# One hybrid block on one core: the output projection as one accumulation of 12 k tiles beside attention and 4 after it

## The chip, the cores and the metric

The kernel runs on one core of a Trainium2 chip. A core has a matrix engine (PE, with its weight loads shown as PEld), a vector engine (DVE), a scalar engine (ACT), a general engine (POOL) and a queue engine (SP) that only issues transfers; transfers are also issued by POOL and ACT. The five run side by side, each in the order of its own instruction list, and meet only at semaphores. The metric is the device time of one execution in microseconds (us): lower is better.

## The reference

The block normalises its input, projects it, runs a state-space mixer (SSD) and a sparse attention side by side, joins their outputs, and projects the joined rows back onto the residual stream. Then a gated feed-forward part and a last normalisation follow. Shapes: 512 positions, model width 2048, SSD and attention 1024 each, feed-forward 5632, all in float32.

```python
u = rmsnorm(h, attn_norm_w)
z, xbc, dt_raw, q, kc, vc, ks, vs, kw, vw, gate_raw = split(u @ w_in)
y_ssd = ssd_mixer(...)        # ends in rmsnorm(y * silu(z), ssd_norm_w)
y_att = nsa_mixer(...)        # 16 heads: compressed, selected and windowed keys
mixed = concatenate([y_ssd, y_att], axis=-1)
h = h + mixed @ w_out                      # the projection of this case
v = rmsnorm(h, ffn_norm_w)
h = h + (silu(v @ w_gate) * (v @ w_up)) @ w_down
return rmsnorm(h, final_norm_w)
```

## The kernel before

Activations lie transposed: a tile holds 128 channels by 512 positions. `mixed` is 16 such k tiles: 8 of SSD (`P2["ms"]`) and 8 of attention (`P2["ma"]`). Each float32 operand is split into a rounded part (`hi`, made by ACT in `a_hi`) and a rest (`lo`, made by DVE). A product of one k tile is three PE instructions: hi with hi, hi with lo, lo with hi.

The first phase is a list of *units* (`run_unit`, L232 to L234). A unit makes one block of 128 output channels: it sums its k tiles into one PSUM bank `ps_g` (two banks take turns). Its weights come through `wp`, a pool with rings of four buffers: SP loads 4 k tiles (256 KB) into `wraw`, ACT makes `whi`, DVE makes `wlo`. After every k tile the code calls `sch.tick()`, and background tasks (generators) get to add their next instructions: the attention heads of group after group, the evictions of earlier units, and so on. What the code writes in this phase is then ordered by the planner of the language, engine by engine, from its own estimate of times; only from the feed-forward part on does the order stand as written.

The projection is cut in two.

- **Units over the SSD half.** The last 16 units (one for each 128 output channels) sum the 8 SSD k tiles, `w_out[c][:, 0:8]`, while the last attention group runs as a background task. `pre_out` runs before the first of them: it loads the gated SSD rows from `gy_d`, multiplies by the norm weight `C_SN` and splits them into `ms`. The division by the root mean square of a position, `row2`, is left to the eviction `ev_os`: DVE multiplies the PSUM block by `row2` into a tile `h1`, POOL's queue adds the residual `xT` in a transfer, and a second transfer writes it to `h1_d`. `ma_in` meanwhile reads back from `at_d` the attention tiles that were finished earlier.
- **Steps over the attention half.** When all tasks are done, `pre_oa` closes the pools of attention (`att`), of the weights (`wp`) and of the constants (`c1`) and opens `ws` in their place: `A`, `Z` (raw weights, 48 slots of 128x128), `R` (split weights), `E`, `T`, `V0`. Then 16 steps (`run_step`, L1154 to L1156) sum the 8 attention k tiles, `w_out[c][:, 8:16]`. The eviction `ev_oa(c)` adds `h1` (read from `h1_d` into a ring of two tiles, `HH`), writes the sum to `h_d`, adds its square to `acc2`, weights it by `C_FN` and splits it into the operands of the feed-forward part. `load_h1(c + 2)` then reads the next `h1` into the tile that step c has just used, and a step's PSUM bank is free when the add of the step two before it is done.

Gate, up and down products follow in the feed-forward part, whose weights stream through `Z` to the end.

Of the kernel before, what the change touches and what calls it, by code (L numbers as in the profile page):

```python
# [8 lines left out]
F32 = mybir.dt.float32  # L9
# [14 lines left out]
          (0, 5), (7, 5), (1, 5), (6, 5), (2, 5), (7, 5), (5, 6), (0, 6), (3, 6), (4, 6), (1, 4), (6, 4), (2, 4),  # L24
          (0, 6), (2, 3), (6, 5), (7, 6), (5, 6), (3, 6), (4, 6), (1, 6)]
GRING = 7
KSUB = 4
PACE = [1]
LAG = 3
# [83 lines left out]
def body(ctx, tc, xT, w_in, w_out, w_gate, w_up, w_down, w1k, w1v, cols, rows, kst, out):  # L113
# [53 lines left out]
    def open_pool(name, stack=None, **kw):  # L167
        es = ExitStack()
        pools[name] = (es, es.enter_context(tc.tile_pool(name=name, bufs=1, reuse_waits="tile", **kw)))
        return pools[name][1]  # L170
# [2 lines left out]
        pools.pop(name)[0].close()  # L173

    c1 = open_pool("c1")
    wp = open_pool("wp")


    subs = []
# [115 lines left out]
    up = right.enter_context(tc.tile_pool(name="up", bufs=1, side="right", reuse_waits="tile"))  # L295

    U = up.tile([128, 2, KD, 512], F32R, name="u")
    u_hi, u_lo = U[:, 0], U[:, 1]

    def u_rhs(k):  # L300
# [655 lines left out]
    def pre_out():  # L956
        sch.run_until(*[("gy", t) for t in range(8)])
        P2["ms"] = [(U[:, 0, k], U[:, 1, k]) for k in range(8)]
        P2["ma"] = [(U[:, 0, 8 + k], U[:, 1, 8 + k]) for k in range(8)]
        for k in range(8):  # L960
            w = col(C_SN + k)
            h_, l_ = P2["ms"][k]
            nc.sync.dma_start(f(l_), gy_d[k])
            a_hi(h_, f(l_), scale=w)
            dve.scalar_tensor_tensor(l_, f(l_), w, f(h_), op0=ALU.mult, op1=ALU.subtract)
        sch.add(ma_in(P2["at"] + 1))

    def ma_in(n):

        yield 8  # L970
        for k in range(n):
            h_, l_ = P2["ma"][k]
            nc.sync.dma_start(f(l_), at_d[k])
            yield 8
            a_hi(h_, f(l_))
            lo(dve, l_, f(l_), h_)

    def ev_os(c):
        def ev(p):
            yield from sch.wait("r2")  # L980
            t = pools["att"][1].tile([128, 512], F32, tag="qs", name="h1", bufs=2)
            mul(dve, t, p, P2["row2"])
            nc.gpsimd.dma_start(t, xT[c], accum_op=ALU.add)
            yield 4
            nc.gpsimd.dma_start(h1_d[c], t)
        return ev

    for c in range(KD):
        units.append(Unit(w_out[c][:, 0:8, :], 8, lambda k: P2["ms"][k], ev_os(c),
                          pre=pre_out if c == 0 else None))  # L990

# [168 lines left out]


    def pre_oa():
        sch.drain()
        close_pool("att")
        close_pool("wp")
        close_pool("c1")
        wsp = open_pool("ws")
        A = P2["A"] = wsp.tile([128, NA, 128], F32, name="A")  # L1170
        P2["T"] = {i: wsp.tile([128, 8, 2, 256], F32R, name=f"T{i}") for i in range(2)}
        P2["Z"] = wsp.tile([128, NZ, 128], F32, name="Z")

        P2["R"] = wsp.tile([128, 8 + NR * 128], F32R, name="R")[:, 8:].rearrange("p (k c) -> p k c", k=NR)
        tp = open_pool("ta", side="right")
        P2["V0"] = tp.tile([128, 8, 2, 256], F32R, name="V0")
        P2["VV"] = U[:, :, 0:8, :].rearrange("p a k (s t) -> p a k s t", s=2)
        at = 8
        for n, k in (("SR", 2), ("TT", 4), ("HH", 4), ("CT", 8), ("ST", 16)):
            P2[n] = A[:, at:at + 2 * k, :].rearrange("p (k a) t -> p k (a t)", a=2)  # L1180
            at += 2 * k
        P2["T34"] = P2["ST"].rearrange("p (a k) t -> p a k t", a=2)
        P2["T2"] = P2["CT"]
        P2["T1"] = [P2["Z"][:, i:i + 8, :].rearrange("p (k a) t -> p k (a t)", a=2) for i in (NZ - 16, NZ - 8)]
        fz.busy[NZ - 16:] = [True] * 16

        P2["E"] = open_pool("E", side="right").tile([128, NE * 128 + 8], F32R, name="E")[:, 0:NE * 128].rearrange(
            "p (k c) -> p k c", k=NE)
        advance()
        load_h1(0)  # L1190
        load_h1(1)

    def load_h1(c):
        if c < KD:
# [3 lines left out]
    def ev_oa(c):  # L1198
        def ev(p):
            h = P2.pop(("h1", c))  # L1200
            add(dve, h, p, h)
            nc.gpsimd.dma_start(h_d[c // 2][:, 2 * (c % 2):2 * (c % 2) + 2, :].rearrange("p a t -> p (a t)"), h)
            t = P2["t", c % 2] = P2["TT"][:, 2 * (c % 2):2 * (c % 2) + 2].rearrange("p a t -> p (a t)")
            dve.tensor_scalar(t, h, col(C_FN + c), None, op0=ALU.mult)
            if c == 0:
                act.activation(acc2, h, AF.Square)
            else:
                q = ps_v()
                act.activation(q, h, AF.Square)
                add(dve, acc2, q, acc2)  # L1210
            k = c // 2
            if c % 2 == 0:
                a_hi(P2["V0"][:, k, 0, :], t[:, 0:256])
                lo(dve, P2["V0"][:, k, 1, :], t[:, 0:256], P2["V0"][:, k, 0, :])
            else:
                e = P2["t", 0]
# [5 lines left out]
                pool.tensor_tensor(P2["T34"][:, 0, k, :], e[:, 256:512], t[:, 256:512], ALU.subtract)  # L1222
# [33 lines left out]
        return get  # L1256

    for c in range(KD):
        b = Blk(8, 1, w_out[c][:, 8:16, :])
        loads.append(b)  # L1260
        Step(b, lambda k: P2["ma"][k], oa_psum(c),
             after=ev_oa(c))


# [400 lines left out]
    def down_before(v, n):  # L1665
        def before():
            if n == 1 and v:
                assert v < NJ - 2 or not any(fz.busy[NZ2:])
                load_h(v + 1)
                P2["A2"] = P2["A"][:, 70:76, :]  # L1670
            elif (v, n) == (0, 0):
                close_pool("E")
                load_h(1)
                P2["E2"] = P2["E"] = open_pool("E", side="right").tile([128, NE, 128], F32, name="E2")
        return before

    last = []
# [34 lines left out]
        done.update(((i, 1), s.i) for i in range(a, b))  # L1712

    def run_rest():
        pre_oa()
# [6 lines left out]
        for n in ("E", "ta", "ws"):  # L1722
            close_pool(n)
        right.close()

# [145 lines left out]
```

## Time and profile before

| what | value |
|---|---|
| three runs, median (lowest to highest) | 2243.71 us (2239.92 to 2244.08) |
| the profiled execution's own time | 2242.56 us |
| its span, first to last instruction | 2240.8 us |
| PE, DVE, ACT busy, share of the span | 97%, 80%, 52% |
| mean granted clock of PE | 0.987 |
| last matmul of a unit, first matmul of a step | 763.8 us, 793.8 us |

Busy is time in which the engine has an instruction in work; a busy PE can still run at half its clock, which the granted clock shows. A row of a group gives the count, the busy time, the mean ns of one, and behind the second bar the idle time of that engine just before them and what ended it. In names buffer numbers are left out: `h_d<-h` is the write to `h1_d` in `ev_os`, `A<-h_d` on SP the load of `h1`, and `h_d<-A` the write in `ev_oa`. The table's last row is from the trace in order of time.

### The profile page before, as it was taken

Reading aid. Unit: us, or ns where it says so; the run is one execution under the profiler, and the core shown is the slowest. Engines: PE = TensorE matmul, PEld = TensorE weight load, DVE = VectorE, ACT = ScalarE, POOL = GpSimd, SP = SyncE. Lnnn points to the kernel's source line nnn. Section 1 sums busy time; section 2 is a strip of 40 time slices with the busy share of each in tenths; the row PEclk is TensorE's granted clock in tenths of the full one; section 3 lists DMA queues with packets and bytes.
Section 4 is the critical chain, followed back from the end, with each engine's and each line's share of the span. In section 5 each row is a group of like instructions: output and inputs, shape, how many; then the busy total and the mean of one; then the engine's idle time right before and its main releaser. Section 6 shows DMA issues by size and latency. Waiting matters only on the chain. (4 is left out here: it accounts for less than half of the span.)

```text
span 2240.8 us, 34941 instructions
## 1 busy us (share of the span) xinstructions
PE 2166.9 (97%) x12892; PEld 1905.9 (85%) x12892; DVE 1795.5 (80%) x2838; ACT 1173.0 (52%) x1944; POOL 418.3 (19%) x432
## 2 busy tenths in 40 slices
PE   7999999999989989999999999999999899999996
PEld 5888888888878768888888888888888799999996
DVE  7799766678887656888888888888888798888897
ACT  4564446567666534655555555555556343433453
POOL 2011225133232124100000000000000122212232
PEclk8999999999999989999999999999999999999998
DMA  5222342222325365788878888788888969696975
GB/s 179 90 71 76 117 154 91 85 79 71 123 74 145 71 209 176 217 236 217 247 220 254 226 231 237 215 247 229 238 236 219 331 238 317 180 299 176 300 193 135
DMA packets 168555, 417.17 MB, mean 186 GB/s; under 512 B 16592, under 2 KB 23520, under 8 KB 168384
## 3 DMA queue, kind: packets, MB, share of 16 engines
q1 hardware_dynamic: 97472, 248.04, 33.4%
q0 software_dynamic: 28192, 80.91, 18.7%
q10 hardware_dynamic: 42720, 85.99, 10.6%
q8 instruction: 101, 1.65, 0.3%
q14 instruction: 70, 0.57, 0.1%
HBM read 353.80 MB, written 57.41 MB: 184 GB/s over the span
## 5 line engine op out<-in xcount | busy, mean ns | idle before, releaser
L122 ACT ACTIVATE R<-Z 128x1024 fp32r<-128x1024 f32 (+4 forms) x462 | 423.7, 932 | 463.6 <-DVE Z L134 317.5
L125 DVE TENSOR_TENSOR R<-Z,R 128x1024 fp32r<-128x1024 f32 (+4 forms) x370 | 391.7, 1067 | 24.1 <-ACT R L122 20.7
L232 PE MATMUL ps_g<-u,whi 128*128 128x512 f32 x720 | 286.0, 397 | 0.0
L234 PE MATMUL ps_g<-u,wlo 128*128 128x512 f32 x720 | 284.5, 395 | 0.0
L233 PE MATMUL ps_g<-u,whi 128*128 128x512 f32 x720 | 284.5, 395 | 0.0
L1150 PE MATMUL ps_s<-u,R 128*128 128x512 f32 (+1 forms) x1160 | 252.8, 348 | 5.2 <-ACT A L1357 5.0
L1150 PEld LDWEIGHTS ps_s<-u,R 128*128 128x128 f32 x1160 | 187.7, 188 | 36.9 <-ACT A L1357 10.2
L125 DVE TENSOR_TENSOR wlo<-wraw,whi 128x512 fp32r<-128x512 f32 x196 | 149.6, 765 | 65.1 <-ACT whi L122 64.3
L122 ACT ACTIVATE whi<-wraw 128x512 fp32r<-128x512 f32 x196 | 122.6, 626 | 136.2 <-PE ps_g L233 89.3
L234 PEld LDWEIGHTS ps_g<-u,wlo 128*128 128x128 f32 x720 | 135.7, 188 | 26.6
L232 PEld LDWEIGHTS ps_g<-u,whi 128*128 128x128 f32 x720 | 135.9, 189 | 25.4
L233 PEld LDWEIGHTS ps_g<-u,whi 128*128 128x128 f32 x720 | 135.8, 189 | 25.5
L134 DVE TENSOR_TENSOR A<-ps_g,A 128x512 f32<-128x512 f32 (+1 forms) x114 | 73.9, 654 | 78.1 <-PE ps_g L1150 38.9
L1150 PE MATMUL ps_t<-u,R 128*128 128x512 f32 (+1 forms) x600 | 131.5, 348 | 0.0
L1150 PE MATMUL ps_g<-u,R 128*128 128x512 f32 x584 | 131.3, 349 | 0.0
L1150 PE MATMUL ps_s<-T,R 128*128 128x512 f32 (+1 forms) x560 | 126.9, 352 | 1.7 <-DVE R L125 1.7
L1150 PE MATMUL ps_g<-T,R 128*128 128x512 f32 (+1 forms) x584 | 127.2, 349 | 0.2 <-DVE R L125 0.2
L1154 PE MATMUL ps_g<-u,R 128*128 128x256 f32 (+1 forms) x353 | 115.2, 326 | 10.6 <-ACT R L122 7.0
L1150 PE MATMUL ps_s<-V,R 128*128 128x512 f32 (+1 forms) x568 | 122.7, 347 | 0.0
L122 ACT ACTIVATE R<-A 128x1024 fp32r<-128x1024 f32 (+3 forms) x76 | 72.1, 949 | 96.5 <-DVE A L134 59.9
L125 DVE TENSOR_TENSOR E<-Z,R 128x1024 fp32r<-128x1024 f32 x92 | 112.1, 1218 | 5.6 <-ACT R L122 5.2
L1155 PE MATMUL ps_g<-u,R 128*128 128x256 f32 (+1 forms) x353 | 114.4, 324 | 0.0
(473 smaller groups left out, 5633.8 us busy)
## 6 DMA issues: line engine op xcount, KB each, us to landing
Z<-in_w_up SPq DMA_DIRECT2D x95, 512.0 KB, 5.3
Z<-in_w_gate SPq DMA_DIRECT2D x94, 512.0 KB, 6.6
wraw<-in_w_in SPq DMA_DIRECT2D x164, 256.0 KB, 2.6
g_d<-A ACTq DMA_DIRECT2D x22, 1792.0 KB, 15.2
Z<-in_w_gate POOLq DMA_DIRECT2D x38, 512.0 KB, 6.6
Z<-in_w_up POOLq DMA_DIRECT2D x38, 512.0 KB, 8.7
Z<-in_w_down SPq DMA_DIRECT2D x59, 320.0 KB, 5.9
Z<-in_w_down SPq DMA_DIRECT2D x41, 384.0 KB, 4.0
```

The costliest lines, as they stand in the source:

```text
L122: act.activation(dst, src, AF.Copy, scale=scale)
L125: eng.tensor_tensor(dst, src, f(hi), ALU.subtract)
L134: eng.tensor_tensor(o, a, b, ALU.add)
L232: pe.matmul(p, hi_t[i][:, j, :], ah, start=(k == 0), stop=False)
L233: pe.matmul(p, hi_t[i][:, j, :], al, start=False, stop=False)
L234: pe.matmul(p, lo_t[i][:, j, :], ah, start=False, stop=(k == u.nk - 1))
L1150: pe.matmul(o, w, x, start=start, stop=(k == n - 1 and o is q), skip_group_check=not fresh[0])
L1154: pe.matmul(q, h[:, k, :], ah, start=(k == 0), stop=False)
L1155: pe.matmul(q, h[:, k, :], al, start=False, stop=False)
```

## The change

- `NS = 12`: a unit of the projection now sums 12 k tiles, the 8 of SSD and the first 4 of attention (48 weight loads for the 16 units in place of 32); a step sums the last 4, in blocks of 256 KB.
- Since one sum now holds both halves, `row2` cannot wait for the eviction. `pre_out` applies it to the operand: one DVE instruction multiplies by the norm weight and by `row2`, ACT makes `hi`, and one more DVE instruction makes `lo`. The rows come through the ring `wraw` of `wp`. `ev_os` is then a copy by ACT, into one tile `yz` where two tiles `qs` took turns.
- `wp` lies at the other end of memory (on the right, beside `u`), so that it can stay open when the pools of the left end change.
- `pre_last` runs ahead of the last unit: it takes all of attention's remaining instructions, closes `att` and `c1`, opens `ws` and issues the first loads of the steps; `first_forms` splits the first two blocks 6 and 9 ticks into the last unit. `T` moves to the place of `wp` and `V0` and `E` to the left end.
- In `ev_oa` the weighting by `C_FN` moves from DVE (L1204) to ACT.

```diff
+NS = 12
...
-    wp = open_pool("wp")
...
+    wp = open_pool("wp", side="right")
...
         for k in range(8):
-            w = col(C_SN + k)
             h_, l_ = P2["ms"][k]
-            nc.sync.dma_start(f(l_), gy_d[k])
-            a_hi(h_, f(l_), scale=w)
-            dve.scalar_tensor_tensor(l_, f(l_), w, f(h_), op0=ALU.mult, op1=ALU.subtract)
+            t = wp.tile([128, 512], F32, tag="raw", name="gy", bufs=4)
+            nc.sync.dma_start(t, gy_d[k])
+            dve.scalar_tensor_tensor(t, t, col(C_SN + k), P2["row2"], op0=ALU.mult, op1=ALU.mult)
+            a_hi(h_, t)
+            lo(dve, l_, t, h_)
...
     def ma_in(n):
-        yield 8
         for k in range(n):
...
-            yield 8
+            yield 1 if k < NS - 8 else 8
...
     def ev_os(c):
         def ev(p):
-            yield from sch.wait("r2")
-            t = pools["att"][1].tile([128, 512], F32, tag="qs", name="h1", bufs=2)
-            mul(dve, t, p, P2["row2"])
+            if "att" in pools:
+                t = pools["att"][1].tile([128, 512], F32, tag="yz", name="h1", bufs=1)
+            else:
+                t = P2["TT"][:, 2 * (c % 2):2 * (c % 2) + 2].rearrange("p a t -> p (a t)")
+            act.activation(t, p, AF.Copy)
             nc.gpsimd.dma_start(t, xT[c], accum_op=ALU.add)
...
+    def pre_last():
+        sch.run_until(("a", 3), ("evac", st["unit"]))
+        pre_oa()
+        sch.add(first_forms())
+
+    def first_forms():
+        yield 6
+        prep(0)
+        yield 3
+        prep(1)
...
-        units.append(Unit(w_out[c][:, 0:8, :], 8, lambda k: P2["ms"][k], ev_os(c),
-                          pre=pre_out if c == 0 else None))
+        units.append(Unit(w_out[c][:, 0:NS, :], NS, os_rhs, ev_os(c),
+                          pre={0: pre_out, KD - 1: pre_last}.get(c)))
...
-            dve.tensor_scalar(t, h, col(C_FN + c), None, op0=ALU.mult)
+            a_hi(t, h, scale=col(C_FN + c))
...
-        b = Blk(8, 1, w_out[c][:, 8:16, :])
+        b = Blk(16 - NS, 1, w_out[c][:, NS:16, :])
...
-        Step(b, lambda k: P2["ma"][k], oa_psum(c),
+        Step(b, lambda k: P2["ma"][NS - 8 + k], oa_psum(c),
```

Three places in the built programs follow. The PE list is the same in both up to the start of the projection.

The first is ACT where attention ends and the steps begin. `fo<-ps_v` and `u<-at` belong to the last attention tile, and `R<-Z` is the first split of a step's weights. Before:

```order
L122 ACTIVATE pth<-ps_t 128x2x128
L122 ACTIVATE pth<-ps_t 128x3x128
L122 ACTIVATE pth<-ps_t 128x4x128
L884 ACTIVATE fo<-ps_v 64x512
L122 ACTIVATE u<-at 128x512
L122 ACTIVATE R<-Z 128x1024 x4
```

And now, with the last unit's eviction `A<-ps_g` added:

```order
L124 ACTIVATE pth<-ps_t 128x2x128
L124 ACTIVATE pth<-ps_t 128x3x128
L124 ACTIVATE pth<-ps_t 128x4x128
L886 ACTIVATE fo<-ps_v 64x512
L124 ACTIVATE u<-at 128x512
L988 ACTIVATE A<-ps_g 128x512
L124 ACTIVATE R<-Z 128x512 x4
```

The first splits stand behind the last attention tile in both. In both programs the first load into `Z` also waits for the DVE instruction that writes that tile `at`, since `Z` lies over the tiles of `att`.

The second is SP from the last unit's weights on. `A<-h_d` is `load_h1`. Before:

```order
L198 DMA wraw<-in_w_out 128x512 x20
L1089 DMA Z<-in_w_out 128x1024 x4
L1089 DMA A<-in_w_out 128x1024
L1196 DMA A<-h_d 128x512 x2
L1089 DMA Z<-in_w_out 128x1024 x4
L1196 DMA A<-h_d 128x512
```

And now:

```order
L199 DMA wraw<-in_w_out 128x512 x32
L1111 DMA Z<-in_w_out 128x512 x8
L1111 DMA A<-in_w_out 128x512 x2
L1220 DMA A<-h_d 128x512 x2
L1111 DMA Z<-in_w_out 128x512 x6
L1220 DMA A<-h_d 128x512 x3
```

Ten loads of 256 KB stand ahead of the first two of `h1` where five of 512 KB stood, and six more stand ahead of the third.

The third is DVE within two steps, from one add of `h1` (`A<-ps_g,A`) on. Before:

```order
L134 TENSOR_TENSOR A<-ps_g,A 128x512
L125 TENSOR_TENSOR R<-Z,R 128x1024
L1204 TENSOR_SCALAR A<-A,colc 128x512
L134 TENSOR_TENSOR acc_95<-ps_v,acc_95 128x512
L125 TENSOR_TENSOR V_8274<-A,V_8274 128x256
L134 TENSOR_TENSOR A<-ps_g,A 128x512
```

And now:

```order
L136 TENSOR_TENSOR A<-ps_g,A 128x512
L127 TENSOR_TENSOR R<-A,R 128x512
L136 TENSOR_TENSOR acc_95<-ps_v,acc_95 128x512
L136 TENSOR_TENSOR A<-ps_g,A 128x512
L127 TENSOR_TENSOR V_8531<-A,V_8531 128x256
```

The weighting is gone from DVE and the split of a block is half as wide; the two adds and the splits of the operand are as before.

More of the change, by code (lines that the diff above doesn't have):

```diff
@@ L960, in pre_out @@
         for k in range(8):
-            w = col(C_SN + k)
             h_, l_ = P2["ms"][k]
-            nc.sync.dma_start(f(l_), gy_d[k])
-            a_hi(h_, f(l_), scale=w)
-            dve.scalar_tensor_tensor(l_, f(l_), w, f(h_), op0=ALU.mult, op1=ALU.subtract)
+            t = wp.tile([128, 512], F32, tag="raw", name="gy", bufs=4)
[3 more added lines that the diff above has]
+            lo(dve, l_, t, h_)
+        assert P2["at"] >= NS - 9, P2["at"]
         sch.add(ma_in(P2["at"] + 1))
     def ma_in(n):
-        yield 8
         for k in range(n):
@@ L973, in ma_in @@
             nc.sync.dma_start(f(l_), at_d[k])
-            yield 8
+            yield 1 if k < NS - 8 else 8
             a_hi(h_, f(l_))
             lo(dve, l_, f(l_), h_)
+            sch.flags.add(("ma", k))
     def ev_os(c):
         def ev(p):
-            yield from sch.wait("r2")
-            t = pools["att"][1].tile([128, 512], F32, tag="qs", name="h1", bufs=2)
-            mul(dve, t, p, P2["row2"])
+            if "att" in pools:
[3 more added lines that the diff above has]
+            act.activation(t, p, AF.Copy)
             nc.gpsimd.dma_start(t, xT[c], accum_op=ALU.add)
@@ L986, in ev_os, with os_rhs @@
         return ev
+    def os_rhs(k):
+        if k >= 8:
+            assert ("ma", k - 8) in sch.flags
+        return (P2["ms"] + P2["ma"])[k]
+    def pre_last():
[7 more added lines that the diff above has]
+        prep(1)
     for c in range(KD):
-        units.append(Unit(w_out[c][:, 0:8, :], 8, lambda k: P2["ms"][k], ev_os(c),
-                          pre=pre_out if c == 0 else None))
+        units.append(Unit(w_out[c][:, 0:NS, :], NS, os_rhs, ev_os(c),
+                          pre={0: pre_out, KD - 1: pre_last}.get(c)))
     class Blk:
@@ L1164, in pre_oa @@
     def pre_oa():
-        sch.drain()
         close_pool("att")
-        close_pool("wp")
         close_pool("c1")
@@ L1170, in pre_oa @@
         A = P2["A"] = wsp.tile([128, NA, 128], F32, name="A")
-        P2["T"] = {i: wsp.tile([128, 8, 2, 256], F32R, name=f"T{i}") for i in range(2)}
         P2["Z"] = wsp.tile([128, NZ, 128], F32, name="Z")
         P2["R"] = wsp.tile([128, 8 + NR * 128], F32R, name="R")[:, 8:].rearrange("p (k c) -> p k c", k=NR)
-        tp = open_pool("ta", side="right")
-        P2["V0"] = tp.tile([128, 8, 2, 256], F32R, name="V0")
+        P2["V0"] = wsp.tile([128, 8, 2, 256], F32R, name="V0")
         P2["VV"] = U[:, :, 0:8, :].rearrange("p a k (s t) -> p a k s t", s=2)
@@ L1185, in pre_oa @@
         fz.busy[NZ - 16:] = [True] * 16
-        P2["E"] = open_pool("E", side="right").tile([128, NE * 128 + 8], F32R, name="E")[:, 0:NE * 128].rearrange(
+        P2["E"] = open_pool("E").tile([128, NE * 128 + 8], F32R, name="E")[:, 0:NE * 128].rearrange(
             "p (k c) -> p k c", k=NE)
@@ L1191, in pre_oa, with pre_steps @@
         load_h1(1)
+    def pre_steps():
+        sch.drain()
+        close_pool("wp")
+        tp = open_pool("ta", side="right")
+        P2["T"] = {i: tp.tile([128, 8, 2, 256], F32R, name=f"T{i}") for i in range(2)}
     def load_h1(c):
@@ L1673, in before @@
                 load_h(1)
-                P2["E2"] = P2["E"] = open_pool("E", side="right").tile([128, NE, 128], F32, name="E2")
+                P2["E2"] = P2["E"] = open_pool("E").tile([128, NE, 128], F32, name="E2")
         return before
@@ L1714, in run_rest @@
     def run_rest():
-        pre_oa()
+        pre_steps()
         for s in steps[:KD]:
@@ L1721, in run_rest @@
             sch.drain()
-        for n in ("E", "ta", "ws"):
+        for n in ("ta", "E", "ws"):
             close_pool(n)
```

## The prediction

> **What bounds the kernel now.** I read the slices of the span first, then the stages around the projection, then what ends PE's idle time there. In the 40 slices (56 us each) PE's clock falls in the fifteenth alone, the first and the last aside:
>
> ```profile
> PE   7999999999989989999999999999999899999996
> PEclk8999999999999989999999999999999999999998
> ```
>
> That is 784 to 840 us, where attention has just ended; the twelfth, 616 to 672, has idle PE too. The view by stages (busy us and count for PE, PEld, DVE, ACT, POOL, then the granted clock, DMA share and GB/s) cuts that place at the last unit's end (764.2), the change of clock (777.5), the first load of the steps (788.2), their first matmul (793.7) and their end (885.7):
>
> ```profile
> 590.00:620.00 30.00, 30.00 (x149) 25.38 (x149) 25.14 (x64) 22.43 (x51) 5.21 (x7) 1.00 0.56 180
> 620.00:655.00 35.00, 28.24 (x151) 22.80 (x150) 31.13 (x96) 24.87 (x66) 10.80 (x11) 0.90 0.12 37
> 655.00:764.20 109.20, 109.17 (x569) 92.91 (x567) 77.00 (x226) 62.82 (x157) 27.40 (x35) 1.00 0.52 126
> 764.20:777.50 13.30, 10.11 (x61) 7.94 (x60) 10.78 (x42) 10.31 (x30) 1.43 (x2) 1.00 0.20 40
> 777.50:788.20 10.70, 8.01 (x25) 5.96 (x25) 3.47 (x7) 2.50 (x7) 0.00 (x0) 0.50 0.00 0
> 788.20:793.70 5.50, 0.00 (x0) 0.00 (x0) 0.69 (x1) 1.63 (x2) 0.00 (x0) 0.50 0.77 235
> 793.70:798.00 4.30, 4.19 (x9) 2.90 (x10) 3.68 (x3) 2.81 (x4) 0.00 (x0) 0.51 0.99 371
> 798.00:885.70 87.70, 87.70 (x376) 70.70 (x376) 53.64 (x76) 33.93 (x48) 34.78 (x46) 1.00 0.66 201
> ```
>
> PE is the bound wherever projection work is there to fill it: 109.17 of 109.20 us in the units, all of 87.70 us in the steps. Between them, from 764.2 to 793.7, attention runs alone on its own chain of waits, and half of that at half clock. The timeline shows how it ends (start, length, engine, what, and the idle time before it):
>
> ```profile
> 763.79 0.39 PE L234 MATMUL ps_g<-u,wlo 128*128 128x512 f32 x1
> ...
> 786.82 0.59 ACT L884 ACTIVATE fo<-ps_v 64x512 f32<-64x512 f32 x1 [3.00 <-PE ps_v L876]
> 787.44 0.69 DVE L134 TENSOR_TENSOR at<-ps_v,fo 64x512 f32<-64x512 f32 x1 [2.90 <-ACT fo L884]
> 788.20 1.75 SPq L1089 DMA_DIRECT2D Z<-in_w_out  x4
> 792.66 1.06 ACT L122 ACTIVATE R<-Z 128x1024 fp32r<-128x1024 f32 x1 [3.87 <-DMA Z<-in_w_out]
> 793.77 0.80 PE L1154 MATMUL ps_g<-u,R 128*128 128x512 f32 x1 [6.99 <-ACT R L122]
> ```
>
> The steps' first load leaves 0.07 us after DVE's add of the last attention tile (787.44 + 0.69 = 788.13), because its memory was attention's; ACT's split waits for it, and PE for the split, 6.99 us in all.
>
> **The change, part by part.**
>
> *The moved matmuls.* 16 blocks x 4 k tiles x 3 = 192 go from the steps to the units. A step's matmul costs 87.70 / 376 = 0.233 us, so 44.7 us leave the steps; in the units they cost at most as much. I take 0 (at best 1 us less).
>
> *The tail is covered.* From 764.2 to 793.7 are 29.5 us. Its work at full clock is 10.11 + 8.01 / 2 = 14.1 us, so 15.4 us are idle or lost to the clock. In the new order the last unit's matmuls stand between attention's, down to its last transposes. But the wait behind them stays: the first `Z` load still waits for the add of the last tile, so `first_forms`, written into the last unit, cannot run there. What remains is 786.82 to 788.20 (1.4 us), one load, and a split of half the width. These transfers (KB each, median us from issue to landing) and splits bear on it and on the next parts:
>
> ```profile
> wraw<-in_w_out SPq DMA_DIRECT2D x31, 256.0 KB, 3.1
> Z<-in_w_out SPq DMA_DIRECT2D x13, 512.0 KB, 5.1
> h<-in_xT POOLq DMA_DIRECT2D x16, 256.0 KB, 4.8
> h_d<-h POOLq DMA_DIRECT2D x16, 256.0 KB, 2.5
> A<-h_d SPq DMA_DIRECT2D x16, 256.0 KB, 3.5
> h_d<-A POOLq DMA_DIRECT2D x16, 256.0 KB, 2.6
> ```
> ```profile
> L122 ACT ACTIVATE whi<-wraw 128x512 fp32r<-128x512 f32 x24 | 15.0, 625 | 8.8 <-PE ps_g L233 5.5 <-issue 3.2
> ```
>
> The load takes 3.1 us (median for 256 KB) to 4.5 us (788.20 to 792.66, the first of a burst); 1.4 + 3.5 + 0.6 = 5.5 us, nearer the short end since the block is half as large. Gain: 15.4 - 5.5 = 9.9 us (9.0 to 10.3).
>
> *Evictions in the units.* DVE's product becomes ACT's copy, 0.6 us like the split above, on engines that have room (DVE 77.00, ACT 62.82 of 109.20 us). The one tile `yz` turns in 0.6 + 4.8 + 2.5 = 7.9 us; a unit has 36 matmuls, 36 x 0.227 = 8.2 us (the row of 763.79 starts 0.23 us after the one before it) beside attention. Hidden by 0.3 us at the tightest; if it is not, ACT's copy holds the weight splits queued behind it, 0.3 us a unit for the few units after attention. 0 to +2; I take 0.
>
> *`pre_out`.* Eight more DVE instructions of about 0.69 us, 5.5 us, near 600 us, where DVE has 4.9 of 30 us left; behind them is the stage 620 to 655, where PE idles 6.8 us, mostly on DVE:
>
> ```profile
> PE ps_s L831 <- DVE em L835: 5.5, 4, 1.9
> ```
>
> Against it stand more projection matmuls to fill that idle. At worst +5.5 (all on the path), at best -6.8 (all idle filled); I take 0. The `gy` loads share the ring with the weights, whose prefetch is three blocks deep there.
>
> *The steps.* PE needs 12 x 0.233 = 2.8 us a step now, 44.7 us for 16. DVE needs for a pair of steps, from these groups (800 to 880 us):
>
> ```profile
> L134 DVE TENSOR_TENSOR A<-ps_g,A 128x512 f32<-128x512 f32 x14 | 9.7, 691 | 29.7 <-PE ps_g L1156 22.4 <-DMA A<-h_d 7.3
> L134 DVE TENSOR_TENSOR acc<-ps_v,acc 128x512 f32<-128x512 f32 x12 | 8.2, 680 | 0.0
> L1204 DVE TENSOR_SCALAR A<-A,colc 128x512 f32<-128x512 f32 x13 | 6.7, 519 | 0.6 <-POOL A L1222 0.6
> L125 DVE TENSOR_TENSOR u<-A,u 128x512 fp32r<-128x512 f32 x6 | 4.2, 692 | 0.6
> L125 DVE TENSOR_TENSOR V<-A,V 128x256 fp32r<-128x256 f32 x7 | 4.1, 588 | 0.5 <-ACT V L122 0.5
> ```
>
> 2 x 0.69 + 2 x 0.68 + 0.69 + 0.59 + 2 x 0.69 for the two splits = 5.4 us, 2.7 a step with L1204 gone to ACT: as full as PE. But the ring of `h1` is longer than either. Add, write of `h_d`, load of the `h1` two steps on, next add: 0.69 + 2.6 + 3.5 + three hand-overs of 0.05 = 6.9 us a pair, 3.5 a step, and PSUM's two banks hold PE to the adds. Before, a pair had 11.2 us of matmuls to hide it; even so DVE waited 7.3 us for such loads. A step now moves 0.75 MB (block, `h1`, write), in 3.6 us 208 GB/s ahead of any prefetch, where the stage from 798 shows 201 with it: transfers will not be quicker than these medians, and I take 7.2 a pair. The ends of the two transfers' ranges:
>
> ```profile
> L1196 SPq DMA_DIRECT2D A<-h_d x16: 326/327/540, 790.6 to 882.2; - x16
> ...
> DMA to landing us min/median/max: 2.5/3.5/8.7
> ```
> ```profile
> L1202 POOL DMA_DIRECT2D h_d<-A x16: 542/562/895, 802.8 to 889.2; - x16
> ...
> DMA to landing us min/median/max: 2.3/2.6/7.0
> ```
>
> The first `h1` load stands behind 2.6 MB of weights, as before: the 8.7 us, which put the first add some 6.5 us after the first matmul. So 6.5 + 7 x 7.2 + 2.8 = 59.7 us, 15.0 over PE's 44.7. The half-clock restart (4.30 us at 0.51, 2.1 us lost) now falls into that first wait: -2.1. Bounds: pair at its shortest, 0.69 + 2.3 + 2.5 = 5.5 (47.8 us, +3.1), and at 8.5 (68.8 us, +24).
>
> *The clock.* Stalls of 2 us can cost clock:
>
> ```profile
> 640.90:644.30 3.40, 1.09 (x7) 0.56 (x5) 3.33 (x14) 1.25 (x4) 3.32 (x5) 1.00 0.03 5
> 644.30:647.80 3.50, 3.50 (x14) 3.08 (x13) 3.44 (x10) 3.39 (x9) 2.40 (x4) 0.51 0.08 14
> ...
> 893.50:896.90 3.40, 1.92 (x11) 1.34 (x9) 3.34 (x3) 0.91 (x2) 0.34 (x1) 1.00 0.42 145
> 896.90:900.30 3.40, 3.19 (x18) 2.84 (x19) 3.40 (x5) 2.66 (x5) 0.96 (x2) 1.00 0.97 200
> ```
>
> PE busy for a third of 3.4 us was followed by half clock, busy for 56% was not. Steps that are busy 2.8 of 3.6 us on average stay above that, with one lump below: +1.7 (0 to +8). The Trainium skill, "TensorE: Matmul & The Clock Gate", HAM oscillation, has the rule as no idle gaps over about 3.4 us; by it the steps' stalls would cost no clock and the sum would be 1.7 lower. The rows at 640.9 disagree: gaps of under 2 us there were followed by half clock.
>
> *The start of the feed-forward part.* Its first splits and the pieces of `T` queue on a DVE that has had no slack; before, the stage around 893.5 idles PE 1.5 us already. 0 to +4; +2.
>
> Sum: -9.9 + 15.0 - 2.1 + 1.7 + 2 = +6.7, of which the moved matmuls may give back up to 1: I forecast +6. Against the profiled 2242.56 us (a span of 2240.8 and 1.8 around it) that is 2248.6; the median of the runs is 1.15 above the profiled one, so 2249 to 2250. I say 2249.
>
> **The rivals.** *Faster: the ring hides.* If write and load land near their shortest, a pair takes 5.5 us and the steps 47.8: -9.9 + 3.1 - 2.1 + 0 + 1 = -8, 2236. It decides at the pair: each 0.1 us is 0.7 us in the total, and the sum is zero at a pair of 6.3. For it: isolated loads do reach 2.5. Against: the median of 3.5 and the 7.3 us of waits under half the load.
> *No change: write at its median, load quick.* 0.69 + 2.6 + 2.5 + 0.15 = 5.9 a pair, 50.6 us: -9.9 + 5.9 - 2.1 + 1 + 2 = -3, 2241. The Trainium skill, "DMA: Bandwidth & Descriptors", Anatomy of one DMA, prices a transfer at 2.0 us and its bytes over 436 GB/s, 2.6 us for 256 KB, by which the ring would be such; the write's row agrees, the load's 3.5 does not. The gap at the end vanishing altogether (a `Z` tile freed early) would end near here too: +6 - 5.5.
> *Slower still: the steps run at half clock.* 12 matmuls then take 5.6 us, more than the ring, and recover only after a full busy window; four to five windows more at 1.7 us add 8: 2257.
>
> **How the numbers follow.** Forecast 0.45, ring hidden 0.15, no change 0.22, half clock 0.18. 0.2% is 4.5 us, about what a measurement of this kernel tells from none. Slower takes the half clock and most of the forecast, whose own range is 2246 to 2255: 0.53; within 0.30; faster 0.17. The range runs from the hidden ring to a little beyond the half clock: 2236 to 2260.
>
> **What would show it.** After: the last projection matmul some 50 us later than 764, the 44 moved and attention's work between; behind attention's last add a `Z` load and 5 to 6 us of idle PE; DVE's add in the steps waiting for `A<-h_d`, and steps of 3.5 to 3.8 us; half-clock windows among them. I am wrong if the steps take 2.8 us each, if PE is busy across attention's end, or if the units, not the steps, show new idle time.

## The result and the profile after

The changed kernel takes 2255.12 us (median of 7 runs, 2249.01 to 2259.01) against 2241.34 us before (7 runs, 2237.59 to 2244.08): ratio 1.0062 [1.0047, 1.0077], so 13.8 us slower where 6 were forecast. Its profiled execution took 2257.57 us, 1.8 of it around a span of 2255.8, 15.0 longer than the span before.

In the slices of the span (56 us each) PE's dip in the twelfth is gone, and the low point is now the fifteenth and sixteenth, 790 to 902 us, for the clock too.

```profile
PE   7999999999999987999999999999999999999997
PEclk9999999999999988999999999999999999999998
```

The view by stages (busy us and count for PE, PEld, DVE, ACT, POOL, then granted clock, DMA share, GB/s) is cut at the last unit's end (815.7), the first matmul of the steps (824.5) and their end (898.9):

```profile
625.00:660.00 35.00, 31.51 (x146) 25.29 (x146) 31.15 (x91) 25.34 (x62) 9.53 (x10) 0.90 0.35 103
660.00:815.70 155.70, 155.70 (x801) 132.76 (x800) 91.42 (x269) 88.47 (x217) 26.74 (x33) 1.00 0.41 111
815.70:824.50 8.80, 2.57 (x15) 1.73 (x13) 2.11 (x4) 2.93 (x5) 0.87 (x1) 0.79 0.27 84
824.50:898.90 74.40, 58.32 (x206) 43.52 (x206) 43.23 (x60) 36.79 (x62) 32.73 (x44) 0.86 0.66 213
898.90:912.00 13.10, 9.25 (x44) 7.49 (x43) 11.38 (x14) 7.88 (x12) 6.39 (x8) 0.87 0.29 102
```

The units run without a hole, with attention covered down to its last matmuls: 29.5 us between last unit and first step have become 8.8. Its end is as forecast, one short load behind DVE's last addition (start, length, engine, what, and the idle time before it):

```profile
819.84 0.69 DVE L136 TENSOR_TENSOR at<-ps_v,fo 64x512 f32<-64x512 f32 x1 [1.97 <-ACT fo L886]
820.59 4.21 SPq L1111 DMA_DIRECT2D Z<-in_w_out  x8
823.81 0.63 ACT L124 ACTIVATE R<-Z 128x512 fp32r<-128x512 f32 x1 [2.13 <-DMA Z<-in_w_out]
824.50 0.80 PE L1176 MATMUL ps_g<-u,R 128*128 128x512 f32 x1 [5.32 <-ACT R L124]
```

The time is lost in the steps: 74.4 us for 192 matmuls, which PE could do in 44.7. What is waited for there (total us, times, longest):

```profile
DVE A L136 <- DMA A<-h_d: 15.1, 10, 3.5
PE ps_g L1176 <- DVE A L136: 14.9, 8, 3.7
```

DVE's addition waits for the reload of `h1`, and PE, with two banks, for DVE's addition. The additions themselves (start, length, idle before):

```profile
833.63 0.69 DVE L136 TENSOR_TENSOR A<-ps_g,A 128x512 f32<-128x512 f32 x1 [3.46 <-DMA A<-h_d]
834.83 0.68 DVE L136 TENSOR_TENSOR A<-ps_g,A 128x512 f32<-128x512 f32 x1
843.51 1.41 DVE L136 TENSOR_TENSOR A<-ps_g,A 128x512 f32<-128x512 f32 x2 [1.16 <-DMA A<-h_d]
...
865.89 0.69 DVE L136 TENSOR_TENSOR A<-ps_g,A 128x512 f32<-128x512 f32 x1
872.66 0.69 DVE L136 TENSOR_TENSOR A<-ps_g,A 128x512 f32<-128x512 f32 x1 [0.56 <-DMA A<-h_d]
881.41 0.69 DVE L136 TENSOR_TENSOR A<-ps_g,A 128x512 f32<-128x512 f32 x1 [2.15 <-DMA A<-h_d]
...
887.91 0.69 DVE L136 TENSOR_TENSOR A<-ps_g,A 128x512 f32<-128x512 f32 x1
...
898.31 0.69 DVE L136 TENSOR_TENSOR A<-ps_g,A 128x512 f32<-128x512 f32 x1 [1.22 <-DMA A<-h_d]
```

The first comes 9.1 us after the first matmul. From there seven pairs take 898.31 - 833.63 = 64.7 us, 9.24 a pair: 9.9, 7.0, 8.5, 6.9, 15.5, 6.5 and 10.4. The four quick ones average 7.2; the other three hold 14 us more. In the pair of 15.5 (865.89 to 881.41) a write took 5.6 us and the load behind it 8.0, while gate and up weights were loading. The other two long pairs are less a matter of slow transfers. In the pair of 10.4 (887.91 to 898.31) write and load took 3.1 and 2.6 us, but the write left 3.7 us after its addition had ended, because POOL, which issues it, was still at its work for the step before:

```profile
888.55 0.56 POOL L1226 DMA_DIRECT2D h_d<-A  x1 [4.79 <-DVE acc L136]
...
889.83 1.75 POOL L1247 TENSOR_TENSOR A<-Z,A 128x256 f32<-128x256 f32 x1
891.66 0.74 POOL L1248 TENSOR_TENSOR A<-A 128x256 f32<-128x256 f32 x1
892.34 0.56 POOL L1226 DMA_DIRECT2D h_d<-A  x1
```

In the pair of 9.9 (833.63 to 843.51) the write had landed by 838.3 us, but the load of `h1` left at 840.10: on SP a weight's load stood ahead of it, which waited until 839.6 for a split by DVE. Over all the steps, the medians from issue to landing are:

```profile
A<-h_d SPq DMA_DIRECT2D x16, 256.0 KB, 3.4
h_d<-A POOLq DMA_DIRECT2D x16, 256.0 KB, 3.2
```

### The profile page after: what moved, and what is told of

It is laid out like the page before. It is cut to its first block, busy times and chain, and to the rows that moved or that the text cites. A ratio compares the mean times of both kernels' runs of the same rounds, so it can differ in the third digit from the quotient of the medians.

```text
span 2255.8 us, 35038 instructions
## 1 busy us (share of the span) xinstructions
PE 2169.0 (96%) x12892; PEld 1908.7 (85%) x12892; DVE 1789.8 (79%) x2830; ACT 1192.4 (53%) x1992; POOL 417.0 (18%) x432
## 3 DMA queue, kind: packets, MB, share of 16 engines
q0 software_dynamic: 28192, 80.91, 18.2%
## 5 line engine op out<-in xcount | busy, mean ns | idle before, releaser
L124 ACT ACTIVATE R<-Z 128x1024 fp32r<-128x1024 f32 (+4 forms) x449 | 408.7, 925 | 428.1 <-DVE Z L136 302.2
L233 PE MATMUL ps_g<-u,whi 128*128 128x512 f32 x784 | 311.5, 398 | 0.9 <-ACT u L124 0.9
L234 PE MATMUL ps_g<-u,whi 128*128 128x512 f32 x784 | 310.4, 396 | 0.6 <-DVE u L127 0.6
L235 PE MATMUL ps_g<-u,wlo 128*128 128x512 f32 x784 | 310.8, 396 | 0.0
L127 DVE TENSOR_TENSOR wlo<-wraw,whi 128x512 fp32r<-128x512 f32 x212 | 161.7, 765 | 78.7 <-ACT whi L124 78.1
L234 PEld LDWEIGHTS ps_g<-u,whi 128*128 128x128 f32 x784 | 148.0, 189 | 29.4 <-DVE u L127 1.6
L235 PEld LDWEIGHTS ps_g<-u,wlo 128*128 128x128 f32 x784 | 148.0, 189 | 29.1
L233 PEld LDWEIGHTS ps_g<-u,whi 128*128 128x128 f32 x784 | 147.7, 189 | 29.3 <-ACT u L124 1.4
L1172 PE MATMUL ps_g<-u,R 128*128 128x512 f32 (+1 forms) x608 | 131.5, 346 | 0.0
L1172 PEld LDWEIGHTS ps_t<-u,R 128*128 128x128 f32 x608 | 99.0, 188 | 14.1
L1172 PEld LDWEIGHTS ps_g<-u,R 128*128 128x128 f32 x608 | 99.0, 188 | 14.1
L136 DVE TENSOR_TENSOR Z<-Z 128x1024 f32<-128x1024 f32 (+3 forms) x99 | 107.4, 1085 | 3.0 <-POOL Z L136 1.1
```

Source lines behind the costliest of these rows:

```text
L124: act.activation(dst, src, AF.Copy, scale=scale)
L127: eng.tensor_tensor(dst, src, f(hi), ALU.subtract)
L136: eng.tensor_tensor(o, a, b, ALU.add)
L233: pe.matmul(p, hi_t[i][:, j, :], ah, start=(k == 0), stop=False)
L234: pe.matmul(p, hi_t[i][:, j, :], al, start=False, stop=False)
L235: pe.matmul(p, lo_t[i][:, j, :], ah, start=False, stop=(k == u.nk - 1))
```

## The experiments

The theory (A): two `h1` tiles are too few. Each carries an addition, a write to memory and a reload before it is free again, and that round trip, not PE, sets a pair of steps. Rivals: the feed-forward weights' loads take the DMA engines (B); half clock or DVE (C); other parts of the change (D). Each time below is a median; each ratio is to the kernel before on the same chip (2243.8 us, 2243.7 and 2241.6 in the three groups of runs).

### Four tiles

```
+ P2["HX"] = [A[:, i:i + 4, :] ... for i in (20, 24, 8, 0)]
+ az.busy[0:4] = [True] * 4            # freed again when the steps are done
- load_h1(0); load_h1(1)               + for c in range(4): load_h1(c)
- load_h1(c + 2)                       + load_h1(c + 4)
```

> After with the two h1 tiles of the steps made four: the sums of a block go to one of four tiles, and the h1 of block c + 4 instead of c + 2 is loaded behind the write of block c. Theory A (the ring of two is too short: add 0.7, write 3, load 3.5, wait, 9.2 us a pair): a block then has two pairs of time for its round trip, the ring's 9.2 us are spread over four blocks, PE (2.8 us a step) and the splits become the bound; the sixteen steps fall from 74 to 58 to 63 us and the whole is 10 to 14 us under the changed kernel, 0 to 4 us over the kernel before (ratio 1.000 to 1.002). Theory B (the loads of the feed-forward weights take the DMA engines from the ring): half of it, since more loads in flight still stand behind those weights: 4 to 8 us under the changed kernel. Theory C (the steps are held by the halved clock of TensorE or by VectorE): within 3 us of the changed kernel, ratio 1.005 to 1.007.

2247.56 us, 1.0014 [1.0000, 1.0029]: some 11 us of the 14 are back. In the profile the stretch of the steps falls from 74.4 to 58.2 us and DVE's wait for `h1` from 15.1 to 3.0. A holds, and C, which forecast at most 3 us, is out: the edit does not touch the clock or DVE's work. (The clock in the steps rose to 0.94 with most of the stalls gone.) But 16 us in the steps gave 11 in all. At 920 to 940 us PE now waits 3.8 us once for the split of a late weight, a wait of 0.2 in the kernel before, and the down projection, from its first addition out of `ps_g` at 1751.9 us to its last at 2226.9, takes 475.0 us, 3.1 more than the changed kernel's 471.9, each from one execution.

### 10 k tiles beside attention, 6 behind

```
- NS = 12
+ NS = 10
```

> After with NS = 10: 10 k tiles of the output projection beside attention and 6 behind it, nothing else. A step is then 18 matmuls, 4.1 us of PE at full clock, a pair of steps 8.2, and 21.8 us of matmuls move from the units to the steps. Theory A (ring of 9.2 us a pair): the steps stay at 70 to 76 us while the units end 21.8 us earlier, which attention's end gives back by about 10 (its idle time is no longer covered): 4 to 12 us under the changed kernel, ratio to before 1.000 to 1.004. Theory B (the feed-forward weights disturb the ring): the same sign but half, 2 to 6. Theory C (half clock in the steps because PE is idle in them): PE is busy 90% of a step, the clock stays, and the gain is that of A or larger. Theory D (the other parts of the change, the ScalarE evictions, the row on the operand and the pools, cost the time): no change against the changed kernel, 1.005 to 1.007.

2244.91 us, 1.0005 [0.9994, 1.0017]: the 13 us are gone with one number changed. The additions go at 8.4 us a pair up to 852 us, which is PE's part of a pair (36 matmuls), and at 10.3 a pair behind it, where the gate and up weights load: 69.6 us from first to last, about as before the edit (69.1). The steps' clock is now 0.98, so half clock has little part in the pairs of 10.3:

```profile
812.20:888.80 76.60, 74.27 (x312) 58.95 (x313) 50.17 (x67) 44.51 (x69) 34.45 (x47) 0.98 0.76 236
DVE A L136 <- DMA A<-h_d: 7.6, 6, 1.9
```

So it is a question of where the matmuls serve as cover: beside attention they cover its waits, in the steps they cover the ring. At 10 the two are about balanced. (The later weights lie elsewhere too, but it is not there that the time is won: the last addition of the steps comes 14.6 us earlier than in the changed kernel, 888.1 against 902.7, the last of the down projection 15.5.)

### 8 and 8, with all the rest of the change

```
- NS = 12
+ NS = 8
```

> After with NS = 8: the split of the accumulation as it was before, 8 and 8, while the row on the operand, the ScalarE evictions, the weighting by ScalarE, the pools at the other end and the opening of the steps' pools in the last unit stay. Theory A: the steps take PE's 88 to 92 us again and the idle time of attention's end is back, so the time is that of before within 6 us (ratio 0.998 to 1.003). Theory D (the other parts cost what was lost): as the changed kernel or slower, ratio 1.004 to 1.008; the place to look at is the last unit, which waits for attention's third part and opens the pools of the steps, and the first weights behind it.

2262.30 us, 1.0086 [1.0063, 1.0108], 18 us over the kernel before and, by the ratios, some 5 over the changed one, whose interval overlaps this one. This is a miss for A as I had put it, and D is right here. The steps take the 91.8 us of before, but their first matmul comes at 810.9 instead of 793.8. From 560 us to it both kernels issue the same 1109 matmuls; before first, then this one, the whole stretch and the stage behind the last unit:

```profile
560.00:793.77 233.77, 215.53 (x1109) 180.64 (x1108) 173.44 (x496) 143.14 (x356) 53.79 (x64) 0.95 0.39 105
764.20:793.70 29.50, 18.12 (x86) 13.90 (x85) 14.94 (x49) 14.44 (x37) 1.43 (x2) 0.72 0.23 62
```
```profile
560.00:810.86 250.86, 222.55 (x1109) 181.24 (x1108) 166.49 (x488) 149.87 (x372) 53.56 (x63) 0.95 0.35 95
770.40:810.86 40.46, 26.43 (x130) 19.95 (x129) 23.09 (x82) 23.90 (x62) 1.44 (x2) 0.80 0.18 46
PE ps_g L233 <- ACT h L988: 4.8, 4, 2.0
```

PE is idle 28.3 us instead of 18.2, and its matmuls take 7.0 us more, at the same mean clock (0.95). Before, 86 matmuls stood behind the last unit; here 130, because less of attention is issued beside the units. And units wait 4.8 us for ACT's eviction, likely because its single tile does not come round in a unit of 24 matmuls. The changed kernel pays neither: units of 36 matmuls leave 15 in that stage, and no such wait is seen. Of its split, therefore, the cover was worth more than the kernels' plain difference says: from 8 to 12 the first step moves by 13.6 us for 43.6 us of matmuls (192 at 0.227), a gain of 30; the steps (91.8 to 74.2) take back 26 of it.

### The feed-forward weights held back

```
  def advance():
      while nxt["raw"] < len(loads):
+         if nxt["raw"] >= KD and ("oa", 8) not in sch.flags: return
...
+         if KD <= nxt["raw"] < KD + 40 and ("oa", KD - 1) not in sch.flags:
+             dve.tensor_copy(b.ap()[:, 0, 0:1], acc2[:, 0:1])
```

> After with the first gate and up weights of the feed-forward part held back until the sum of squares of block 8 is there (a one-column copy by VectorE into each of their tiles makes their loads wait), so that fewer of their 512 KB loads run beside the h1 ring. Theory B (those weights take the DMA engines from the ring): the pairs of 15.5 and 10.4 us go back to 7 to 8, the steps fall by 6 to 10 us, and the whole by 4 to 8 if the weights still come in time. Theory A (the round trip itself): the pairs before the weights, 7 to 10 us each, stay; the whole is within 3 us of the changed kernel, or up to 5 slower by late weights.

2255.56 us, 1.0068 [1.0047, 1.0089]: as the changed kernel. The additions of the first eight blocks go at 7.7 us a pair (834.3 to 865.0), the later ones, beside the weights, at 10.3 (865.0 to 896.0). The long pairs were moved, not removed; what is held back has to come before the steps end. The pairs are longer where the weights load, here as with `NS = 10`, which speaks for B as what stretches the round trip, though how much of it is transfers and how much the queues that issue them was not followed in these runs; delaying the weights is no cure.

### 10 k tiles with four tiles

```
- NS = 12                  + NS = 10, and the four tiles above
```

> The two edits that paid, together: NS = 10 and four h1 tiles. With NS = 10 alone the pairs of steps stayed at 9.3 us (69.7 us for the adds of 15 steps) though PE needs 8.2. Theory A (the ring of two sets that): with four tiles the steps run at PE's 4.1 to 4.3 us, 15 of them in 62 to 65 us, and the whole is 4 to 7 us under NS = 10 alone, 2238 to 2241, ratio 0.997 to 0.999. Rival (at NS = 10 something else holds the steps, ScalarE's splits or the clock): the adds stay at 4.6 us each and the whole within 2 us of NS = 10 alone, ratio 1.000 to 1.001.

2251.86 us, 1.0033 [1.0022, 1.0045]: slower than NS = 10 alone by 7, a miss by 11. In the profile the steps do run at PE's rate (4.2 us each, no wait for `h1`, first feed-forward matmul on `T` at 889.1 instead of 891.7 us). The loss lies far behind: first to last addition of the down projection, 1748.6 to 2227.9, are 479.3 us, where NS = 10 takes 470.6.

### Two more units, or earlier loads of h1

Blocks 0 and 1 were taken out of the steps altogether, their last 4 k tiles done as units behind the sixteen:

```
+ for c in range(2):
+     units.append(Unit(w_out[c][:, NS:16, :], 16 - NS, lambda k: P2["ma"][NS - 8 + k], tail_ev(c)))
- for c in range(KD):                  + for c in range(2, KD):    # the steps
```

> After, with the last 4 k tiles of blocks 0 and 1 taken out of the steps and put behind the sixteen units as two more units, whose weights come through the units' own pool and need nothing of attention's memory. That fills the 8.5 us between attention's last matmuls and the first step, in which PE is idle 5.3 us. The idea that the gap costs its 5.3 us: 3 to 6 us under the changed kernel, ratio 1.004 to 1.005. The theory that the ring of h1 sets the end of the steps: the first h1 loads come when attention's memory is free, with or without the two units, the ring of two then runs as long as before from there, so what the units do early is waited for later: within 2 us of the changed kernel or up to 3 slower, 1.005 to 1.007.

2264.19 us, 1.0085 [1.0065, 1.0105]: by the ratios some 5 us over the changed kernel, above what either theory gave, though the interval reaches down to the second. The gap at attention's end is filled, and a longer one stands behind it:

```profile
835.19 0.69 DVE L136 TENSOR_TENSOR A<-ps_g,A 128x512 f32<-128x512 f32 x1 [6.02 <-DMA A<-h_d]
836.03 0.77 PE L1186 MATMUL ps_g<-u,R 128*128 128x512 f32 x1 [7.39 <-DVE A L136]
```

PE has both banks full and waits 7.4 us for the first addition, which waits for the first `h1`. That supports A: work done early in front of the ring is waited for in it. Whether it is really slower than the changed kernel, and by what, stays open: the two intervals overlap.

The other attempt put the first two `h1` loads ahead of 2 MB of weights:

```
  nxt["raw"] += 1
+ if nxt["raw"] == 2: load_h1(0); load_h1(1)
```

> After, with the first two loads of h1 put on SP's queue behind the first two weights of the steps, ahead of the other eight (2 MB), behind which they stood. In the profile the first add came 9.1 us after the first step's matmul, waiting for that load. Theory A (the ring sets the end, so its start counts in full): the first add comes 3 to 5 us earlier, all later ones with it, and the whole falls by 3 to 5 us, ratio 1.004 to 1.005. Rival (the weights are next in line: delayed by 512 KB, they hold the steps): the first add earlier, the last where it was, within 1.5 us of the changed kernel.

2259.02 us, 1.0061 [1.0043, 1.0079]: no gain in the timed runs. In its profile the first addition is 3.2 us earlier and the last 6.2, but that execution was the quickest of its six (2251.09 us), and the profiled one of the changed kernel among the slower of its own. This stays open within 4 us.

### Three tiles, placed where no weight lies

The four-tile kernels had taken four places of the weights' staging area, and all weights behind came to lie in other tiles. With three tiles, every load of a gate, up or down weight has the same place and turn as in the changed kernel.

```
+ P2["HX"] = [A[:, i:i + 4, :] ... for i in (20, 24, 8)]
- load_h1(c + 2)                       + load_h1(c + 3)
```

> After with three h1 tiles instead of two. The three lie where no weight is ever placed, so that every load of a gate, up or down weight keeps the tile that it has in the changed kernel; the four tiles of the earlier run took four places of the weights' staging area during the steps, and all later weights of that kernel came to lie elsewhere. Theory A (the round trip of 9.2 us for each tile sets the steps): three blocks in 9.2 us, 3.1 us a step, near PE's 2.8 to 3.0; 15 adds in 46 to 52 us instead of 69; the whole 12 to 16 us under the changed kernel, ratio 0.999 to 1.001. If four tiles are needed: pairs of 7.5 us and more, 4 to 8 us under the changed kernel, 1.003 to 1.004. If what the steps gain is given back in the feed-forward part wherever its weights lie: as with four tiles, 1.001 to 1.002.

2244.03 us, 1.0005 [0.9994, 1.0017]: one more tile and nothing else brings back the whole loss, as A had it.

```profile
825.40:890.80 65.40, 53.48 (x210) 40.03 (x211) 51.02 (x66) 40.56 (x68) 35.04 (x47) 0.95 0.78 250
DVE A L136 <- DMA A<-h_d: 6.5, 4, 2.2
```

The steps take 65.4 us against 74.4, the clock in them is 0.95 against 0.86. The fifteen intervals between the additions take 55.2 us, more than the 46 to 52 expected: 3.3 a step up to 861 us, 4.2 after it, where the weights load.

### What the placement costs

```
  NS = 10, two tiles
+ az.busy[0:4] = [True] * 4            # freed when the steps are done; nothing lies there
```

> NS = 10 with two h1 tiles, and the four places of the staging area that four tiles took are kept empty during the steps: the ring as in NS = 10, the places of all later weights as in NS = 10 with four tiles. Theory P (placement costs): steps as in NS = 10 (9.3 us a pair), the down part 476 to 480 us instead of 470.6, the whole 6 to 11 us over NS = 10, ratio 1.003 to 1.005. Rival (the four-tile run lost its time otherwise): as NS = 10, 0.9995 to 1.0015.

2253.41 us, 1.0061 [1.0042, 1.0081]: with the ring of NS = 10, and the four places merely empty, the loss is there. And NS = 10 with three tiles, which leaves the places alone:

> NS = 10 with three h1 tiles; again all later weights lie as in NS = 10 with two. NS = 10 with four tiles had its steps 3.8 us shorter in the profile and was yet 7 us slower, the loss being behind 1748 us, in the down projection. Theory P (the loss came from where the weights lie, not from the ring): with three tiles the steps gain 3 to 5 us (4.2 us a step, 62 to 64 for the adds) and keep it: 2239 to 2242, ratio 0.998 to 0.9995. Rival (a shorter stretch of steps is given back later whatever is done): 1.000 to 1.004.

2236.62 us, 0.9983 [0.9975, 0.9992]: faster than both kernels, 4 to 5 us under before and some 18 under the changed one. Its steps run at PE's rate, DVE never waiting for `h1`:

```profile
811.60:885.10 73.50, 73.48 (x307) 58.97 (x308) 49.99 (x67) 44.42 (x67) 34.56 (x47) 0.96 0.77 248
L136 DVE TENSOR_TENSOR A<-ps_g,A 128x512 f32<-128x512 f32 x16 | 11.0, 689 | 12.8 <-PE ps_g L1178 12.8
```

The down projection takes 469.0 us here (1745.9 to 2214.9) and 480.3 with the empty places (1752.8 to 2233.1). What PE waits for there, three tiles first, then two tiles without empty places, then with them:

```profile
PE ps_t L1178 <- DVE R L127: 3.1, 4, 2.3
PE ps_g L1178 <- DVE R L127: 3.1, 7, 0.7
```
```profile
PE ps_t L1178 <- DVE R L127: 4.8, 7, 2.5
PE ps_g L1178 <- DVE R L127: 4.2, 8, 1.0
PE ps_s L1178 <- DVE R L127: 1.0, 4, 0.4
```
```profile
PE ps_g L1178 <- DVE R L127: 6.4, 12, 1.2
PE ps_t L1178 <- DVE R L127: 4.8, 9, 2.2
PE ps_s L1178 <- DVE R L127: 3.3, 6, 1.4
```

The same waits for weight splits, more and longer. The cleanest pair is `NS = 10` with two tiles, without and with the empty places (1.0005 and 1.0061): the ring's code is the same, and in the built programs 178 of the 198 loads of down weights have another place or turn. The steps end at the same time (888.1 us), the part from there to the down projection takes 861.4 and 864.7 us, the down projection 470.7 and 480.3. In the latter PE idles 6.8 us more, of which these waits are 4.5; where the rest comes from is open. So a choice of tiles at 820 us was paid for at 1800 to 2200, and the miss of `NS = 10` with four tiles has its cause: the down weights of that kernel have the places and turns of the one with empty places (1.0033 and 1.0061), and three tiles, which leave the places alone, gain (0.9983). Which weight comes late by which tile was not followed.

### Two candidates

NS = 11, blocks 0 and 1 as units, with four tiles and with three:

> A version meant to beat both: NS = 11 (11 k tiles beside attention, 5 behind), four h1 tiles, and the last 5 k tiles of blocks 0 and 1 as two more units that fill attention's end. By theory A no ring wait is left: 14 steps of PE's 3.4 us, the gap at attention's end mostly filled: 5 to 12 us under the changed kernel with four tiles (2247.6), 2236 to 2242, ratio 0.996 to 0.999. If the start of the feed-forward part (weights that come later than the steps need them) takes the place of the ring, it ends where the four tiles alone did, 1.000 to 1.002.

2242.43 us, 0.9999 [0.9986, 1.0012]: level with the kernel before, at the edge of the expectation. Its last addition in the steps is 12.1 us earlier than before (876.2 against 888.3), its last of the down projection 1.1 (2218.9 against 2220.0). One wait for a weight split at the start of the feed-forward part is 3.7 us of what lies between; the rest is spread over it.

> The version meant to beat both, once more, with three h1 tiles instead of four: NS = 11 and the last 5 k tiles of blocks 0 and 1 as units behind the sixteen. With four tiles its steps ended 12 us before those of the kernel before, and 3.7 us were lost at 920 to 940 us where PE waited for the split of a late weight. Theory P: no place is taken from the weights, the late weight comes earlier, 2 to 5 us under the four-tile version: 2237 to 2240, ratio 0.9975 to 0.999. Rival (the feed-forward part gives the gain back wherever its weights lie): 2241 to 2244, 0.999 to 1.0005.

2248.56 us, 1.0029 [1.0018, 1.0039]: slower, against both expectations. Two late steps take 12.0 us (870.6 to 882.6), and only 1.4 us of it is a wait for `h1`: POOL stands still for 5.9 us ahead of a weight's load that it issues, ACT then waits 3.6 us for POOL's next work, and DVE 3.3 us for ACT. The down part takes 473.9. With another number of steps every place differs again; the placement may be the cause, and no run here shows it.

## Why the prediction was right in sign and short in size

Counted by its own steps, from the two profiles:

| term | forecast | measured |
|---|---|---|
| first step, against 44.7 us of matmuls moved ahead of it | -9.9 | 30.7 - 44.7 = -14.0 |
| steps: ring, half-clock restart, clock | +15.0 - 2.1 + 1.7 = +14.6 | 74.2 - (91.8 - 44.7) = +27.1 |
| feed-forward part and behind | +2 | +1.8 |
| sum | +6.7 | +14.9 |

*The moved matmuls and the covered tail.* Right in kind: the last projection matmul is 52 us later, and the wait that stays is 5.32 us where 5.5 were worked out. The 4 us more come from terms put at 0: the stage of 625 to 660 us idles PE 3.5 us instead of 6.8, and the moved matmuls cost 0.227 us, not 0.233.

*Evictions and `pre_out` at 0.* Right for this kernel, where 12 k tiles cover them; at 8, the same edits and the order of attention that comes with them cost 17 us at the first step.

*The steps: the term that was mis-sized.* Place, cause and waits were as forecast, the length was not: first addition at 9.1 us instead of 6.5, pairs of 9.24 instead of 7.2 (above the bound of 8.5 too), an end of 0.4 instead of 2.8. The first addition is late because the first `h1` load left SP 5.5 us after the first weight (820.59 to 826.12), behind ten loads, where it had been 2.4 us behind five (788.20 to 790.61); it then took 7.4 us.

The 7.2 was a chain of medians (6.9) with 0.3 added, and the four quick pairs average 7.2. But the ring adds up every trip, and nothing gives a long trip back. In the 64.7 us of the seven pairs, followed one by one, the seven writes take 23.1 us and the seven loads 26.4, 49.5 where the forecast's medians give 42.7; the seven additions take 4.8. The other 10.4 us are hand-overs, 1.5 a pair where 0.15 were forecast. Already the shortest, from the end of an addition to POOL's issue of the write, is 0.3 us, and the long ones are time that a transfer stands in the queue of its engine, the 3.7 us on POOL and the 1.8 on SP above. So the hand-overs were missed by more (9.3 us) than the transfers (6.8). The forecast had the long landings in its rows (7.0 and 8.7 at most) and kept them for the first load alone. It also argued that the transfers would not be *quicker* than before, without pricing that they could be slower beside the weights; in one later run they were quicker (below). Its traffic figure was a little low: 0.75 MB a step is 0.79 with 256 KB as 128 x 512 x 4 bytes, 218 GB/s and not 208.

*The clock.* One half-clock window, +1.7, was forecast; the clock fell four times behind the restart, the steps' clock is 0.86, and five windows of 3.4 us ran at half clock (below), as many as the rival "half clock" named. It cost little all the same, because the time that half clock takes is time in which PE would have waited for the ring: PE is idle 16.1 of the 74.4 us, and the additions waited 15.1 us for `h1` and on no matmul. Only through the split that SP's load waited for in the first pair could it have reached the ring, for 1.8 us at most. The rival gave 2257 us, near the measured 2255; but with a third tile, an edit that does not touch the clock, time and clock both come back (2244 us, 0.95). The number was near and the windows came, but they did not set the steps.

*The start of the feed-forward part.* +2 forecast, +1.8 as what is left of the span; that the two agree to 0.2 us in single executions is partly luck.

*Luck in the total.* The steps lost 12.5 us more than forecast and the first step won 4.1 more. The two errors come from different stages and happen to offset each other in part, and the total lies within the stated range also because that range was stretched beyond the half-clock rival, whose mechanism is not the one seen.

*The rivals.* "The ring hides" and "no change" needed pairs under 6.3 us; the shortest was 6.5. The Trainium skill, "DMA: Bandwidth & Descriptors", Anatomy of one DMA, states its formula for transfers that POOL issues, as the ring's write is; by it 256 KB take 2.6 us, an estimate. The write's median was 2.6 us before and is 3.2 in the changed kernel. The loads are issued by SP, for which the formula is not stated; they took 2.6 us with the empty places and 3.4 in the changed kernel.

## What to carry to other kernels

Before moving matmuls away from a loop, ask what they cover there: a ring of buffers through memory has a trip time of its own, and when the work per turn falls below it, the ring is the loop. Price such a ring by its mean trip under the traffic of that stage, with its long landings and with the time that its transfers stand in the queues of the engines that issue them, and give it one buffer more before anything else. And where a planner places later data by what is free now, compare variants stage by stage: a variant's total can carry 10 us of placement from a stage that was never edited.

## What the runs showed of the hardware

*Short stalls cost the clock.* Behind the restart the clock falls to half four times in the steps, at 834.4, 844.7, 872.0 and 882.2 us. Each time the 3.4 us before hold 0.7 to 1.2 us of busy PE; the waits for an addition that end near there are 2.51, 2.50, 3.73 and 1.55 us. Three of the four, in the columns of the view by stages:

```profile
831.00:834.40 3.40, 0.96 (x5) 0.43 (x3) 0.77 (x2) 0.68 (x2) 0.00 (x0) 1.00 1.05 401
834.40:837.80 3.40, 3.34 (x8) 2.72 (x9) 1.54 (x3) 3.18 (x6) 2.95 (x5) 0.51 1.00 366
...
868.60:872.00 3.40, 1.17 (x5) 0.59 (x4) 3.40 (x4) 1.62 (x4) 1.64 (x2) 1.00 0.93 251
872.00:878.80 6.80, 5.30 (x12) 3.80 (x12) 2.57 (x5) 1.76 (x3) 3.96 (x5) 0.50 0.97 227
878.80:882.20 3.40, 0.70 (x3) 0.23 (x2) 1.16 (x2) 1.06 (x2) 0.00 (x0) 1.00 0.58 174
882.20:885.60 3.40, 3.40 (x8) 2.73 (x9) 1.72 (x3) 1.73 (x4) 1.34 (x2) 0.51 0.42 154
```

The length of the wait does not decide it alone. Another wait of 2.50 us, from 857.4 to 859.9, cost no clock. The four falls lie whole multiples of about 3.4 us apart; counted in such stretches, that wait is split between two, 854.9 to 858.3 and 858.3 to 861.7, in which PE was still busy 2.47 and 1.83 us.

The Trainium skill, "TensorE: Matmul & The Clock Gate", describes under "A second HAM failure mode: psum-queue depth-cycling" that frequent short idle times between groups of matmuls are enough to make the clock swing; this trace agrees, with PE busy for a fifth to a third of the 3.4 us before each drop.

*Landing times belong to a stage.* The same 256 KB load and write, in the steps of NS = 10 with two tiles, without and with the four empty places (with them, seven gate and up loads were issued in that time instead of eight; whether that is the reason was not tested):

```profile
h_d<-A POOLq DMA_DIRECT2D x16, 256.0 KB, 4.1
A<-h_d SPq DMA_DIRECT2D x14, 256.0 KB, 3.1
```
```profile
h_d<-A POOLq DMA_DIRECT2D x16, 256.0 KB, 3.2
A<-h_d SPq DMA_DIRECT2D x14, 256.0 KB, 2.6
```

Write and load together fall by 1.4 us, and the first thirteen intervals between additions take 55.8 us (819.9 to 875.7), near PE's rate, where the same two tiles without the empty places took 61.6 (818.4 to 880.0).
